# Decoder layer on one core: scaling of h on GpSimd and ScalarE, squares summed first, quarters of six column pairs ahead

## The chip, the cores and the metric

One core of a Trainium2 chip. The metric is the device time of one execution in microseconds (us), the median of three runs. In the text TensorE is PE in the rows, VectorE is DVE, ScalarE is ACT, GpSimd is POOL, and SyncE, which issues the weight loads, is SP.

## What is computed

One hybrid decoder layer on 256 tokens of width 2048, all in float32: a conditioning vector gives six modulation vectors, a normalised and modulated `h` feeds two token mixers (an attention with low-rank projections and an mLSTM), their gated sum goes through an output projection, and a mixture of 32 experts follows. The part that matters here is the beginning:

```python
mod = cond @ w_ada[l] + b_ada[l]
sh_a, sc_a, gt_a, sh_m, sc_m, gt_m = [m[:, None, :] for m in jnp.split(mod, 6, axis=-1)]
h = rmsnorm(x, norm_mix_g[l]) * (1.0 + sc_a) + sh_a
...
proj = h @ w_in
```

`rmsnorm(x, g)` is `x * rsqrt(mean(x * x) + EPS) * g`, and `w_in` is split into the columns of nine projections.

## The kernel before

Activations lie transposed: a block k holds 128 of the 2048 features on the partitions and 256 tokens along the free axis, so there are 16 blocks (`KT`). Weights come from HBM in pieces of 1 MB into the rotating buffers of the pool `big` (nine of them; conditioning vector and the halves of `h` hold some for long). SyncE issues the loads in the order of the program, and each waits until its buffer is free.

**Matmuls in parts.** Most products with `h` are made of three matmuls (`mm3`, L198 to L201): weights and activations are each split into a rounded high part (ScalarE, `split` L186, and `hh`) and a remainder (VectorE, L187, and `hl`). These are the split matmuls. In the first eight blocks (`WHOLE`) the head columns are multiplied in full float32 instead (L810), from `h` itself.

**The start.** ScalarE squares x in eight pieces, and TensorE sums each over the partitions by two products with a matrix of ones (L208); from the sum ScalarE makes `rstd`, the inverse root (L157, L158).

**The head loop** (from L787) goes over the 16 blocks. For block k it loads two rows of `w_ada` (1 MB each) and the head columns of `w_head` (0.7 MB); VectorE multiplies the two rows with the conditioning vector and sums along the free axis (`ada`, L143: a product of 128x2048 and a read of its accumulator), which gives the scale and the shift of the block; then come the gain (`ada_gain`, L151), the shift's bias (`ada_bias`, L146) and the scaling of x by gain and `rstd` (L805) on VectorE, the shift on ScalarE (L808), the high part (L811, ScalarE) and the remainder (L812, VectorE), and eleven products of 128x256 on TensorE. From block 8 on the head columns are split too (`push`), and behind each block stand some of 14 further pieces, `first_halves`: the first eight row blocks of six pairs of query and key columns (`half_pair`, 48 split matmuls each, tile `hp` in PSUM, copied to `part` by ScalarE, L322), of the mLSTM's values (`v_half`, tile `vb`) and of four pairs of output gates. At block 8 the program also emits `rope_tables`, 22 operations on GpSimd that start from the token positions (a load of its own, L348). The second halves are added to `part` later by VectorE (L328).

**What sets the order.** SyncE keeps the order of the program. On the other engines the compiler arranges the instructions at build time, and each engine then executes its list in that order. `push` runs one piece late, so that a split stands ahead of the matmuls that use it.

Of the kernel before, what the change touches and what calls it, by code (L numbers as in the profile page):

```python
# [9 lines left out]
F32 = mybir.dt.float32  # L10
# [63 lines left out]
def decoder_layer_kernel(ctx, tc, xT, c, pos, cols_d, const_d, mask_d, w_ada, w_head, w_half, w_blk, w_mlv, w_pa, w_pb, w_out,  # L74
# [11 lines left out]
    def bank(name):  # L86
        return psum.tile([P, 512], F32, name=name, tag="bank")
# [26 lines left out]
    def col(name, i=0, n=1, p0=0, p1=P):  # L114
        s = COLS[name].start + i
        return cols[p0:p1, s:s + n]
# [19 lines left out]
        act.activation(cond[:, s], b, AF.Silu)  # L136
    pool.memset(lg, NEG)
    vec.tensor_scalar(bada1, col("b_ada", 0, 96), 1.0, None, op0=ALU.add)

    def ada(i):  # L140
        raw = u8("raw")
# [5 lines left out]

    def ada_gain(which, k0, k1, base, g):
        s = slice(base + k0, base + k1)
        if k1 - k0 == 1:  # L150
            vec.tensor_scalar(gs[:, which, k0:k1], mod[:, s], bada1[:, s], col(g, k0), op0=ALU.add, op1=ALU.mult)  # L151
        else:
            vec.tensor_tensor(gs[:, which, k0:k1], mod[:, s], bada1[:, s], op=ALU.add)
            vec.tensor_tensor(gs[:, which, k0:k1], gs[:, which, k0:k1], col(g, k0, k1 - k0), op=ALU.mult)

    def rsqrt(out, ssum, n):
        act.activation(out, ssum, AF.Ln, bias=epsc, scale=1.0 / n)  # L157
# [20 lines left out]
    def pair(name, dt=F32):  # L178
        return by2(t2(name, dt))
# [20 lines left out]
        pe.matmul(out, wh, xl, start=False, stop=False)  # L200
        pe.matmul(out, wl, xh, start=False, stop=last)  # L201

    ssum = bank("ssum")
    for i in range(8):
        sq = pair("sq")
        act.activation(sq, xs[:, 2 * i:2 * i + 2], AF.Square)
        for j in range(2):
            pe.matmul(ssum[:, :T], ones, sq[:, j], start=i + j == 0, stop=i + j == 8)  # L208
    rstd = t2("rstd")
    rsqrt(rstd[:, :T], ssum[:, :T], D)  # L210

# [3 lines left out]
    def hhk(k):  # L215
        return hh[k // 8][:, k % 8]

    def hlk(k):
        return hl[k // 8][:, k % 8]
# [41 lines left out]
    def load(src):  # L261
        raw = u8("raw")
        nc.sync.dma_start(raw, src)
        return raw
# [24 lines left out]
    hblk = [hb[i // 2][:, (i % 2) * T:(i % 2 + 1) * T] for i in range(HEAD_N)]  # L289
    part = {}  # L290

    def half_pair(src, half, after):
        raw = load(src[half])
        b = bank("hp")
        for i in range(2):
            push_block(raw[:, i * 1024:(i + 1) * 1024], b[:, i * T:(i + 1) * T], 8, lambda k: hhk(k + 8 * half),
                       lambda k: hlk(k + 8 * half), (lambda: after(b)) if i else None)

    def v_half(nh, half, after):
        vb = [bank("vb") for _ in range(2)]  # L300
# [31 lines left out]

    def first_halves():
        for i in range(6):
            half_pair(w_half[i], 0, keep_part(("qk", i)))
            yield
        for nh in range(2):
            yield from v_half(nh, 0, keep_part(("v", nh, 0), ("v", nh, 1)))
        for i in range(4):
            half_pair(w_half[6 + i], 0, keep_part(("o", i)))  # L340
            yield
# [445 lines left out]
            push_block(raw[:, i * 1024:(i + 1) * 1024], b[:, i * T:(i + 1) * T], 8, pick(x, 0), pick(x, 1),  # L787
                       (lambda: after(b)) if i else None)

    firsts, n_first = first_halves(), 0  # L790
    for k in range(KT):
        ada(16 + k)
        ada(k)
        raw = u8("raw")[:, :HEAD_N * P]
        nc.sync.dma_start(raw, w_head[k])
        if k == 0:
            nc.sync.dma_start(const, const_d)
        if k == WHOLE:
            rope_tables()
        if k == KT - 1:  # L800
            nc.sync.dma_start(masks, mask_d)
        ada_gain(0, k, k + 1, 16, "mix_g")
        ada_bias(k, k + 1)
        hp = t2("hp")
        vec.scalar_tensor_tensor(hp[:, :T], xs[:, k], gs[:, 0, k:k + 1], rstd[:, :T], op0=ALU.mult, op1=ALU.mult)  # L805
        if k < WHOLE:
            h = hp[:, T:]
            act.activation(h, hp[:, :T], AF.Identity, bias=mod[:, k:k + 1])  # L808
            for j in range(HEAD_N):
                pe.matmul(hblk[j], raw[:, j * P:(j + 1) * P], h, start=k == 0 and j % 2 == 0, stop=False)  # L810
            act.activation(hhk(k), h, AF.Copy)  # L811
            vec.tensor_tensor(hlk(k), h, hhk(k).bitcast(F32), op=ALU.subtract)  # L812
            tick()
            tick()
            continue
        act.activation(hhk(k), hp[:, :T], AF.Identity, bias=mod[:, k:k + 1])
        vec.scalar_tensor_tensor(hlk(k), hp[:, :T], mod[:, k:k + 1], hhk(k).bitcast(F32), op0=ALU.add, op1=ALU.subtract)
        for j0, j1 in ((0, 6), (6, HEAD_N)):
            def fn(wh, wl, j0=j0, j1=j1, k=k):
                for j in range(j0, j1):  # L820
                    s = slice((j - j0) * P, (j - j0 + 1) * P)
                    mm3(hblk[j], wh[:, s], wl[:, s], hhk(k), hlk(k), k == 0 and j % 2 == 0,
                        k == KT - 1 and (j % 2 == 1 or j == HEAD_N - 1))

            push(raw[:, j0 * P:j1 * P], fn, after_head if k == KT - 1 and j1 == HEAD_N else None)
        while n_first < 14 * (k - 7) // 8:
            next(firsts)
            n_first += 1
# [639 lines left out]
def _layout(v):  # L1468
# [14 lines left out]
    head = np.concatenate([cq, ckv, kpe, mi, gap, mf, gap, mqk[:, :P * HEAD_QK]], 1).reshape(KT, P, HEAD_N * P)  # L1483
    two = np.concatenate([mqk[:, P * HEAD_QK:], mlo], 1)
    half = np.stack([blocks(two[:D // 2], 2), blocks(two[D // 2:], 2)], 1)
    blk = np.concatenate([blocks(ga), blocks(gb)], 0)
    mlv = mlv.reshape(4, 4, P, 2, 512).transpose(3, 0, 2, 1, 4).reshape(2, 4, P, 2048)
    uq = f("w_uq")[0].reshape(512, H, 192)
# [70 lines left out]
```

## Time and profile before

| what | before |
|---|---|
| median of 3 runs | 1639.17 us (1639.06 to 1639.73) |
| profiled execution | 1639.2 us, span 1637.3 us |
| TensorE busy | 1378.5 us, 84% |
| VectorE busy | 815.3 us, 50% |
| ScalarE busy | 504.2 us, 31% |
| GpSimd busy | 87.4 us, 5% |
| DMA | 560.96 MB, mean 343 GB/s |
| mean granted TensorE clock | 0.921 |

Busy shares are means over stages with different limits. TensorE's matmuls are pipelined, and a matmul that waits inside the pipeline still counts as busy; so the distance between the starts of matmuls, and the waits of the first one of a group, say more than the share. The granted clock is in parts of full speed: 1.00 is 2.4 GHz, 0.50 is 1.2 GHz.

### The profile page before, as it was taken

The page shows a single profiled execution, that of the slowest core. Times are in us where ns is not written, and L with a number is a line of the kernel's source. Part 1 is how long each engine was busy: PE and PEld are TensorE (multiplying, and loading weights), DVE is VectorE, ACT ScalarE, POOL GpSimd, SP SyncE. Part 2 cuts the span into 40 slices and gives each one's busy share as a digit, 9 for nine tenths or more (in the row PEclk, how much of TensorE's full clock was granted, in tenths as well). Part 3 has the DMA queues.
Part 4 walks back from the last instruction along what each step waited for, and adds up shares of the span by engine and source line. Part 5 has one row for each costly group of instructions (what it writes and reads, how often), then busy time and mean ns, then how long its engine had stood idle before and what let it go on. Part 6 is the DMA issues. An engine that isn't in the chain of part 4 may idle for free.

```text
span 1637.3 us, 24656 instructions
## 1 busy us (share of the span) xinstructions
PE 1378.5 (84%) x9726; PEld 1009.6 (62%) x9726; DVE 815.3 (50%) x1177; ACT 504.2 (31%) x720; POOL 87.4 (5%) x91
## 2 busy tenths in 40 slices
PE   7899998999999999999989689868767656657675
PEld 5698997999999989999747356535413213213212
DVE  5878699879776789986414233224301201201102
ACT  3134765446755574445312121212001001001000
POOL 0150014000000010121000000000000000000000
PEclk9899999999999999999999889998868878888888
DMA  9978767878676779874597999999999999999995
GB/s 383 374 283 329 282 212 283 327 286 296 245 273 242 269 267 416 321 297 155 224 409 273 416 400 378 420 417 393 399 421 422 420 422 421 420 422 421 421 421 228
DMA packets 78462, 560.96 MB, mean 343 GB/s; under 512 B 8705, under 2 KB 8961, under 8 KB 11905
## 3 DMA queue, kind: packets, MB, share of 16 engines
q1 hardware_dynamic: 78050, 558.84, 86.5%
q8 instruction: 80, 1.31, 0.3%
q10 hardware_dynamic: 288, 0.45, 0.1%
q14 instruction: 44, 0.36, 0.1%
HBM read 569.74 MB, written 2.10 MB: 349 GB/s over the span
## 4 chain that ended last, share of the span: by engine, by line
PE 50%; DMA 33%; DVE 6%; ACT 3%; issue 2%; POOL 1%; SPq 0%; DVEq 0%; POOLq 0%; ACTq 0%
DMA ring<-in_w_gu_dram 22%; DMA ring<-in_w_dn_dram 11%; PE gu L1285 6%; PE ga L199 4%; PE yb L1285 4%; PE ga L201 3%; PE ga L200 3%; DVE whl L187 2%; PE hp L201 2%; PE hp L199 2%; PE hp L200 2%; PE xb L1259 2%; PE wo L199 1%; DVE raw L143 1%; PE wo L201 1%
## 5 line engine op out<-in xcount | busy, mean ns | idle before, releaser
L1285 PE MATMUL gu<-ring,xg 128*32 128x512 f32 (+1 forms) x1664 | 270.4, 756 | 138.0 <-DMA ring<-in_w_gu_dram 138.0
L187 DVE TENSOR_TENSOR whl<-raw,whl 128x1024 fp32r<-128x1024 f32 (+1 forms) x222 | 267.1, 1210 | 93.1 <-ACT whl L186 92.6
L186 ACT ACTIVATE whl<-raw 128x1024 fp32r<-128x1024 f32 (+1 forms) x222 | 229.5, 1038 | 255.3 <-PE ga L201 62.7
L1285 PEld LDWEIGHTS gu<-ring,xg 128*32 128x32 f32 (+1 forms) x1664 | 65.7, 136 | 324.6 <-DMA ring<-in_w_gu_dram 172.0
L143 DVE SCALAR_TENSOR_TENSOR raw<-raw,cond 128x2048 f32<-128x2048 f32 x96 | 220.3, 2296 | 16.5 <-DMA raw<-in_w_ada_dram 16.4
L1285 PE MATMUL yb<-ring,aT 128*32 128x512 f32 (+1 forms) x832 | 130.7, 725 | 64.0 <-DMA ring<-in_w_dn_dram 61.9
L199 PE MATMUL ga<-hh,whl 128*128 128x256 f32 x512 | 149.6, 292 | 0.0
L201 PE MATMUL ga<-hh,whl 128*128 128x256 f32 x512 | 145.0, 283 | 1.4 <-DVE whl L187 1.3
L200 PE MATMUL ga<-hl,whl 128*128 128x256 f32 x512 | 144.8, 283 | 0.0
L1285 PEld LDWEIGHTS yb<-ring,aT 128*32 128x32 f32 (+1 forms) x832 | 33.5, 131 | 145.2 <-issue 99.6
L1231 DVE SCALAR_TENSOR_TENSOR xs<-ob,mod,xs 128x256 f32<-128x256 f32 x112 | 46.5, 477 | 131.9 <-PE ob L1325 131.9
L1251 DVE TENSOR_REDUCE wc<-cb 128x1 f32<-128x256 f32 x7 | 3.0, 424 | 215.8 <-PE cb L1248 215.8
L199 PEld LDWEIGHTS ga<-hh,whl 128*128 128x128 f32 x512 | 97.9, 191 | 5.1 <-issue 3.5
L201 PEld LDWEIGHTS ga<-hh,whl 128*128 128x128 f32 x512 | 97.9, 191 | 2.0 <-DVE whl L187 2.0
L200 PEld LDWEIGHTS ga<-hl,whl 128*128 128x128 f32 x512 | 98.0, 191 | 1.0 <-issue 0.7
L187 DVE TENSOR_TENSOR whl<-rawb,whl 128x1024 fp32r<-128x1024 f32 x36 | 43.0, 1221 | 110.7 <-ACT whl L186 110.7
L1303 ACT ACTIVATE s<-gu 128x512 f32<-128x512 f32 x7 | 4.2, 594 | 295.8 <-PE gu L1285 295.8
L201 PE MATMUL hp<-hh,whl 128*128 128x256 f32 x320 | 91.7, 287 | 3.4 <-DVE whl L187 3.3
L199 PE MATMUL hp<-hh,whl 128*128 128x256 f32 x320 | 92.6, 290 | 0.0
L200 PE MATMUL hp<-hl,whl 128*128 128x256 f32 x320 | 91.2, 285 | 0.0
L1314 ACT ACTIVATE yh<-yb 128x512 fp32r<-128x512 f32 x28 | 16.8, 599 | 190.2 <-PE yb L1285 190.2
L186 ACT ACTIVATE whl<-rawb 128x1024 fp32r<-128x1024 f32 x36 | 36.7, 1050 | 122.6 <-DMA rawb<-in_w_gu_dram 59.7
(418 smaller groups left out, 2905.6 us busy)
## 6 DMA issues: line engine op xcount, KB each, us to landing
ring<-in_w_gu_dram SPq DMA_DIRECT2D x208, 1024.0 KB, 14.8
ring<-in_w_dn_dram SPq DMA_DIRECT2D x104, 1024.0 KB, 15.1
raw<-in_w_ada_dram SPq DMA_DIRECT2D x96, 1024.0 KB, 6.8
raw<-in_w_blk_dram SPq DMA_DIRECT2D x32, 1024.0 KB, 5.1
raw<-in_w_half_dram SPq DMA_DIRECT2D x20, 1024.0 KB, 6.9
raw<-in_w_out_dram SPq DMA_DIRECT2D x16, 1024.0 KB, 6.5
raw<-in_w_head_dram SPq DMA_DIRECT2D x16, 704.0 KB, 7.8
rawb<-in_w_gu_dram SPq DMA_DIRECT2D x10, 1024.0 KB, 10.4
```

Of the source, the lines that this page charges most:

```text
L143: vec.scalar_tensor_tensor(raw, raw, 1.0, cond, op0=ALU.mult, op1=ALU.mult, accum_out=mod[:, i:i + 1])
L186: keep(act.activation(hi, raw, AF.Copy))
L187: keep(vec.tensor_tensor(lo, raw, hi.bitcast(F32), op=ALU.subtract))
L199: pe.matmul(out, wh, xh, start=first, stop=False)
L200: pe.matmul(out, wh, xl, start=False, stop=False)
L201: pe.matmul(out, wl, xh, start=False, stop=last)
L1231: vec.scalar_tensor_tensor(xs[:, d], src, mod[:, 80 + d:81 + d], xs[:, d], op0=ALU.mult, op1=ALU.add)
L1251: vec.tensor_reduce(wc, cb[:, :T], axis=AX.X, op=ALU.add)
L1259: pe.matmul(b[:, i * P:(i + 1) * P], xr[tt][:, k * P:(k + 1) * P], gt[tt], start=tt == 0, stop=tt == 1)
L1285: return lambda: pe.matmul(out[j * C:(j + 1) * C, :], x[:, k * P + j * C:k * P + (j + 1) * C], ws[j][:, cut], start=first, stop=stop)
L1303: act.activation(s, gu[0], AF.Silu)
L1314: act.activation(yh, yb, AF.Copy)
```

## The change

Three things are changed.

First, the eight squared pieces are added up on VectorE, and only the sum goes through the products with ones: two instead of sixteen.

Second, in the head loop the three operations on VectorE (gain, bias, scaling) are gone. GpSimd multiplies x with `rstd`, which needs no conditioning; ScalarE makes the gain (as `mod * mix_g + gbias`, with `gbias` made once) and the biased shift, and applies both in one activation. The high part and the remainder of a block are made in the same way in all 16 blocks.

Third, `half_pair` takes quarters: its 1 MB of weights is laid out so that half of it holds four row blocks of both columns. Six quarters (row blocks 0 to 3) run inside the loop behind blocks 4 to 7: one, two, one and two. `first_halves` then runs only row blocks 4 to 7 of these six pairs, and VectorE adds them to `part`.

```diff
+    gbias = keep.tile([P, KT], F32, name="gbias")
+    vec.tensor_tensor(gbias, bada1[:, KT:2 * KT], col("mix_g", 0, KT), op=ALU.mult)
...
-    ssum = bank("ssum")
+    ssum, total = bank("ssum"), None
     for i in range(8):
-        sq = pair("sq")
-        act.activation(sq, xs[:, 2 * i:2 * i + 2], AF.Square)
-        for j in range(2):
-            pe.matmul(ssum[:, :T], ones, sq[:, j], start=i + j == 0, stop=i + j == 8)
+        sq = t2("sq")
+        act.activation(by2(sq), xs[:, 2 * i:2 * i + 2], AF.Square)
+        if total is None:
+            total = sq
+        else:
+            vec.tensor_tensor(total, total, sq, op=ALU.add)
+    for j in range(2):
+        pe.matmul(ssum[:, :T], ones, total[:, j * T:(j + 1) * T], start=j == 0, stop=j == 1)
...
-    def half_pair(src, half, after):
-        raw = load(src[half])
+    def half_pair(src, half, after, quarters=(0, 1)):
+        q0, q1 = quarters[0], quarters[-1] + 1
+        raw = u8("raw")[:, :(q1 - q0) * 1024]
+        nc.sync.dma_start(raw, src[half][:, q0 * 1024:q1 * 1024])
         b = bank("hp")
-        for i in range(2):
-            push_block(raw[:, i * 1024:(i + 1) * 1024], b[:, i * T:(i + 1) * T], 8, lambda k: hhk(k + 8 * half),
-                       lambda k: hlk(k + 8 * half), (lambda: after(b)) if i else None)
+        for q in quarters:
+            def fn(wh, wl, q=q):
+                for i in range(2):
+                    for j in range(4):
+                        k, s = 8 * half + 4 * q + j, slice((4 * i + j) * P, (4 * i + j + 1) * P)
+                        mm3(b[:, i * T:(i + 1) * T], wh[:, s], wl[:, s], hhk(k), hlk(k), q == q0 and i + j == 0,
+                            q == q1 - 1 and i == 1 and j == 3)
+            push(raw[:, (q - q0) * 1024:(q - q0 + 1) * 1024], fn, (lambda: after(b)) if q == q1 - 1 else None)
+
+    def quarter(i):
+        half_pair(w_half[i], 0, keep_part(("qk", i)), (0,))
...
         for i in range(6):
-            half_pair(w_half[i], 0, keep_part(("qk", i)))
+            half_pair(w_half[i], 0, add_part(("qk", i)), (1,))
...
-        ada_gain(0, k, k + 1, 16, "mix_g")
-        ada_bias(k, k + 1)
         hp = t2("hp")
-        vec.scalar_tensor_tensor(hp[:, :T], xs[:, k], gs[:, 0, k:k + 1], rstd[:, :T], op0=ALU.mult, op1=ALU.mult)
+        h = hp[:, T:]
+        pool.tensor_tensor(hp[:, :T], xs[:, k], rstd[:, :T], op=ALU.mult)
+        act.activation(gs[:, 0, k:k + 1], mod[:, 16 + k:17 + k], AF.Identity, bias=gbias[:, k:k + 1], scale=col("mix_g", k))
+        act.activation(mod[:, k:k + 1], mod[:, k:k + 1], AF.Identity, bias=col("b_ada", k))
+        act.activation(h, hp[:, :T], AF.Identity, bias=mod[:, k:k + 1], scale=gs[:, 0, k:k + 1])
+        act.activation(hhk(k), h, AF.Copy)
+        vec.tensor_tensor(hlk(k), h, hhk(k).bitcast(F32), op=ALU.subtract)
         if k < WHOLE:
...
+            if k >= 4:
+                while n_quarter < 6 * (k - 3) // 4:
+                    quarter(n_quarter)
+                    n_quarter += 1
             continue
-        act.activation(hhk(k), hp[:, :T], AF.Identity, bias=mod[:, k:k + 1])
-        vec.scalar_tensor_tensor(hlk(k), hp[:, :T], mod[:, k:k + 1], hhk(k).bitcast(F32), op0=ALU.add, op1=ALU.subtract)
```

How this moves instructions is seen at four places; the lists are the compiled order of an engine, one row per instruction or run of equal ones. On VectorE at the start, after the change: `sq` is the running sum of squares, `raw,mod<-raw,cond` the conditioning product of a row.

```order
L209 TENSOR_TENSOR sq<-sq 128x512 x4
L145 SCALAR_TENSOR_TENSOR raw,mod<-raw,cond 128x2048
L209 TENSOR_TENSOR sq<-sq 128x512 x2
L145 SCALAR_TENSOR_TENSOR raw,mod<-raw,cond 128x2048
L209 TENSOR_TENSOR sq<-sq 128x512
L822 TENSOR_TENSOR hl<-hp,hh 128x256
```

The last addition stands behind the two products of block 0; before, no addition stood there.

On GpSimd, after the change, around block 8: `hp<-xs,rstd` is the new scaling of a block, `pf`, `kq`, `uq` and `pi` are tiles of the rope tables, and `pi` holds the positions.

```order
L817 TENSOR_TENSOR hp<-xs,rstd 128x256 x8
L363 CAST pf<-pi 128x256
L365 TENSOR_SCALAR pf<-pf,cols 128x256
L369 TENSOR_SCALAR kq<-pf 128x256
...
L375 TENSOR_SCALAR trig<-kq 128x256
L372 TENSOR_SCALAR uq<-kq 128x256
L817 TENSOR_TENSOR hp<-xs,rstd 128x256
L373 TENSOR_TENSOR kq<-uq,pf 128x256
L817 TENSOR_TENSOR hp<-xs,rstd 128x256
```

The scalings of blocks 0 to 7 come first; that of block 8 stands behind 15 operations of the rope tables, and those of blocks 9 to 15 between the remaining ones. Before, GpSimd's list held only the rope tables here, and the scaling was VectorE's.

On ScalarE, after the change, from block 4 to block 6: `whl<-raw` is the high part of a quarter's weights, `part<-hp 128x512` the copy of a quarter out of PSUM, `gs`, `mod`, `hp<-hp,mod,gs` and `hh` the gain, shift, application and high part of the next block.

```order
L185 ACTIVATE whl<-raw 128x1024
L818 ACTIVATE gs<-mod,gbias,cols 128x1
L335 ACTIVATE part<-hp 128x512
L819 ACTIVATE mod<-mod,cols 128x1
L820 ACTIVATE hp<-hp,mod,gs 128x256
L821 ACTIVATE hh<-hp 128x256
L185 ACTIVATE whl<-raw 128x1024 x2
L818 ACTIVATE gs<-mod,gbias,cols 128x1
L335 ACTIVATE part<-hp 128x512 x2
L819 ACTIVATE mod<-mod,cols 128x1
```

A quarter's copy stands ahead of the next block's shift. Before, ScalarE's list in these blocks held only the shift and the high part.

On VectorE, after the change, from the remainder of block 8 to that of block 9: `part<-hp,part` is the sum of a pair's two quarters, `whl<-raw,whl 128x768` and `128x640` the remainders of block 9's head weights.

```order
L822 TENSOR_TENSOR hl<-hp,hh 128x256
L145 SCALAR_TENSOR_TENSOR raw,mod<-raw,cond 128x2048
L186 TENSOR_TENSOR whl<-raw,whl 128x1024
L145 SCALAR_TENSOR_TENSOR raw,mod<-raw,cond 128x2048
L341 TENSOR_TENSOR part<-hp,part 128x512
L186 TENSOR_TENSOR whl<-raw,whl 128x768
L186 TENSOR_TENSOR whl<-raw,whl 128x640
L822 TENSOR_TENSOR hl<-hp,hh 128x256
```

The sum of the quarters waits for TensorE and stands in this stretch, where before the block's scaling and gain stood and no sum.

## Rows read from the trace of the kernel before

**Rows 1.** The chain of waits that ended last, shares of the span by engine.

```profile
PE 50%; DMA 33%; DVE 6%; ACT 3%; issue 2%; POOL 1%; SPq 0%; DVEq 0%; POOLq 0%; ACTq 0%
```

**Rows 2.** Stretches: us, busy (x instructions) per engine, granted clock, DMA share, GB/s.

```profile
40.00:60.00 20.00, 17.74 (x71) 14.32 (x70) 16.61 (x24) 2.77 (x6) 0.00 (x0) 0.90 0.99 391
...
80.00:85.00 5.00, 5.00 (x26) 5.00 (x25) 1.78 (x2) 2.02 (x2) 4.58 (x6) 0.52 0.93 387
...
137.00:186.00 49.00, 48.09 (x313) 43.64 (x312) 38.30 (x48) 23.93 (x33) 0.00 (x0) 1.00 0.93 352
```

**Rows 3.** Timeline, block 1: start, duration, instruction, [idle before, releaser].

```profile
22.63 2.29 DVE L143 SCALAR_TENSOR_TENSOR raw<-raw,cond 128x2048 f32<-128x2048 f32 x1
...
24.96 0.27 DVE L151 TENSOR_SCALAR gs<-mod,bada,cols 128x1 f32<-128x1 f32 x1
25.27 0.48 DVE L805 SCALAR_TENSOR_TENSOR hp<-xs,gs,rstd 128x256 f32<-128x256 f32 x1
...
28.00 0.16 DVE L146 TENSOR_TENSOR mod<-mod,cols 128x1 f32<-128x1 f32 x1
...
28.75 5.01 PE L810 MATMUL hb<-hp,raw 128*128 128x256 f32 x22 [1.88 <-ACT hp L808]
...
29.52 2.28 DVE L143 SCALAR_TENSOR_TENSOR raw<-raw,cond 128x2048 f32<-128x2048 f32 x1
```

**Rows 4.** Timeline of TensorE, blocks 8 and 9 and the first `vb`.

```profile
78.96 0.80 PE L199 MATMUL hb<-hh,whl 128*128 128x256 f32 x2 [3.83 <-ACT hh L816]
...
93.37 1.25 PE L199 MATMUL hb<-hh,whl 128*128 128x256 f32 x6 [1.81 <-ACT hh L816]
...
136.67 0.40 PE L311 MATMUL vb<-whl,hh 128*128 128x512 f32 x1
```

**Rows 5.** Timeline of TensorE, split matmuls at the two clocks.

```profile
80.71 0.41 PE L200 MATMUL hb<-hl,whl 128*128 128x256 f32 x1
...
80.92 0.41 PE L201 MATMUL hb<-hh,whl 128*128 128x256 f32 x1
...
85.64 0.28 PE L199 MATMUL hp<-hh,whl 128*128 128x256 f32 x1
...
85.76 0.28 PE L200 MATMUL hp<-hl,whl 128*128 128x256 f32 x1
```

**Rows 6.** Timeline of the start.

```profile
9.59 8.92 PE L208 MATMUL ssum<-sq,ones 128*128 128x256 f32 x32
...
12.28 2.29 DVE L143 SCALAR_TENSOR_TENSOR raw<-raw,cond 128x2048 f32<-128x2048 f32 x1 [9.02 <-DMA raw<-in_w_ada_dram]
```

**Rows 7.** Costliest groups: count, busy us, mean ns, idle before: the splits.

```profile
L187 DVE TENSOR_TENSOR whl<-raw,whl 128x1024 fp32r<-128x1024 f32 (+1 forms) x222 | 267.1, 1210 | 93.1 <-ACT whl L186 92.6
L186 ACT ACTIVATE whl<-raw 128x1024 fp32r<-128x1024 f32 (+1 forms) x222 | 229.5, 1038 | 255.3 <-PE ga L201 62.7
```

**Rows 8.** Lines L328 and L322: duration ns min/median/max, first and last start.

```profile
L328 DVE TENSOR_TENSOR part<-hp,part x10: 679/685/692, 211.0 to 329.7; 128x512 f32<-128x512 f32 x10
L322 ACT ACTIVATE part<-hp x10: 579/598/600, 91.6 to 205.2; 128x512 f32<-128x512 f32 x10
```

**Rows 9.** Timeline of GpSimd, operations 1, 7, 8, 12 and 15 of the rope tables.

```profile
76.12 0.90 POOL L350 CAST pf<-pi 128x256 f32<-128x256 int32 x1 [75.24 <-DMA pi<-in_pos_dram]
...
82.89 0.85 POOL L359 TENSOR_SCALAR uq<-kq 128x256 f32<-128x256 f32 x1
83.83 0.73 POOL L360 TENSOR_TENSOR kq<-uq,kq 128x256 f32<-128x256 f32 x1
...
89.30 3.00 POOL L361 TENSOR_SCALAR kq<-kq 128x256 f32<-128x256 f32 x1
...
94.70 1.19 POOL L359 TENSOR_SCALAR uq<-kq 128x256 f32<-128x256 f32 x1
```

**Rows 10.** Timeline of SyncE, the issue of the positions.

```profile
66.69 0.42 SPq L348 DMA_DIRECT2D pi<-in_pos_dram  x1
```

More of the change, by code (lines that the diff above doesn't have):

```diff
@@ L149, in ada_gain @@
         s = slice(base + k0, base + k1)
[L150 to L154, printed above, removed]
+        vec.tensor_tensor(gs[:, which, k0:k1], mod[:, s], bada1[:, s], op=ALU.add)
+        vec.tensor_tensor(gs[:, which, k0:k1], gs[:, which, k0:k1], col(g, k0, k1 - k0), op=ALU.mult)
     def rsqrt(out, ssum, n):
@@ L788, in proj_gemm @@
                        (lambda: after(b)) if i else None)
-    firsts, n_first = first_halves(), 0
+    firsts, n_first, n_quarter = first_halves(), 0, 0
     for k in range(KT):
@@ L801, in decoder_layer_kernel @@
             nc.sync.dma_start(masks, mask_d)
-        ada_gain(0, k, k + 1, 16, "mix_g")
-        ada_bias(k, k + 1)
         hp = t2("hp")
-        vec.scalar_tensor_tensor(hp[:, :T], xs[:, k], gs[:, 0, k:k + 1], rstd[:, :T], op0=ALU.mult, op1=ALU.mult)
+        h = hp[:, T:]
[5 more added lines that the diff above has]
+        vec.tensor_tensor(hlk(k), h, hhk(k).bitcast(F32), op=ALU.subtract)
         if k < WHOLE:
-            h = hp[:, T:]
-            act.activation(h, hp[:, :T], AF.Identity, bias=mod[:, k:k + 1])
             for j in range(HEAD_N):
                 pe.matmul(hblk[j], raw[:, j * P:(j + 1) * P], h, start=k == 0 and j % 2 == 0, stop=False)
-            act.activation(hhk(k), h, AF.Copy)
-            vec.tensor_tensor(hlk(k), h, hhk(k).bitcast(F32), op=ALU.subtract)
             tick()
             tick()
+            if k >= 4:
+                while n_quarter < 6 * (k - 3) // 4:
+                    quarter(n_quarter)
+                    n_quarter += 1
             continue
-        act.activation(hhk(k), hp[:, :T], AF.Identity, bias=mod[:, k:k + 1])
-        vec.scalar_tensor_tensor(hlk(k), hp[:, :T], mod[:, k:k + 1], hhk(k).bitcast(F32), op0=ALU.add, op1=ALU.subtract)
         for j0, j1 in ((0, 6), (6, HEAD_N)):
@@ L1485, in _layout @@
     half = np.stack([blocks(two[:D // 2], 2), blocks(two[D // 2:], 2)], 1)
+    half = np.ascontiguousarray(half.reshape(10, 2, P, 2, 2, 512).transpose(0, 1, 2, 4, 3, 5)).reshape(10, 2, P, 2048)
     blk = np.concatenate([blocks(ga), blocks(gb)], 0)
```

## The prediction

> **What bounds the kernel now.** I read the chain of waits first, then busy time by stretches, then the timeline of the stretch that the diff touches. The profiled execution took 1639.2 us with a span of 1637.3, so 1.9 us lie around the span; the median of the three runs is 1639.17, and I make the sum against 1639.2. About 0.2%, 3.3 us, is what a measurement of this kernel can tell from no change.
>
> The chain [rows 1] is half TensorE and a third DMA, the DMA part being the expert stage at the end. Everything that the diff touches lies before 137 us. From 137 to 186 us TensorE is busy for 48.09 of 49 us at a granted clock of 1.00 [rows 2], and nothing there waits long; the stages behind it follow from its end. So a delay or a gain in the first 137 us arrives at the end almost one to one, and the question is only when TensorE reaches its first `vb` matmul, which starts at 136.67 us now [rows 4].
>
> Ahead of that TensorE loses time in two ways. In the first eight blocks VectorE sets the pace: one block runs from 22.63 to 29.52 us, 6.89 us [rows 3], with two conditioning products, three small operations and a wait for ScalarE in it, while TensorE works 5.0 us of it and then waits 1.88. DMA is nearly as tight: share 0.99 from 40 to 60 us at 391 GB/s [rows 2]. Then, at the ninth block, TensorE waits 3.83 us until 78.96, and 1.81 more until 93.37 [rows 4]. After a wait it runs at the lower clock: in 80 to 85 us the granted clock is 0.52 [rows 2], that is mostly 1.2 GHz, and split matmuls start 0.21 us apart; from 85 us on, at 2.4 GHz, they start 0.12 us apart [rows 5]. From 78.96 to 136.67 us it issues four split blocks (132 matmuls) and six first halves (288): 420 times 0.12 is 50.4 us of the 57.7. So 7.3 us are lost there.
>
> **The start.** Sixteen products with `ones` go (8.92 us in 32 records, 0.28 each [rows 6]) and two stay, 4 records, 1.1 us. But the last of the seven new additions stands on VectorE behind both products of the first block, as the order shows. The first product starts when its weights land, 12.28 [rows 6]; two products of 2.35 and three additions of 0.65 (an addition of that shape takes 0.68 [rows 8], starting a little closer) end at about 19.2. With 1.1 us of `ones`, the same 2.2 us of ScalarE as now, 0.73 for POOL's scaling (the shortest two-input POOL row [rows 9]) and 0.5 for ScalarE, TensorE's first block starts at 24.0 instead of 21.86: **2.1 us later**. This part gives nothing back, because those products were hidden beside the conditioning weights.
>
> **Blocks 1 to 4.** VectorE loses 0.27, 0.48 and 0.16 us per block [rows 3]. Its block would be two products of 2.33 start to start, then ScalarE's shift, scale and copy, about 6.3 us. DMA does not follow: 2.8 MB per block at the present rate leaves about 6.7. So 0.2 us per block come back, and h of the fifth block (k = 4) is ready near 50.2 us against 48.9 now.
>
> **Quarters.** One is 24 split matmuls, 24 x 0.12 = 2.9 us at 2.4 GHz; six are 17.3 us of TensorE work taken from behind the ninth block. On ScalarE each quarter's copy out of PSUM (0.60 us [rows 8]) stands ahead of the next block's shift and scale, so the next block cannot start before the quarter ends: 0.6 + 0.2 + 0.5, about 1.4 us of idle TensorE. By that: block 4 at 50.7 to 55.7, quarter to 58.6; block 5 at 60.0 to 65.0, two quarters to 70.8; block 6 at 72.2 to 77.2, quarter to 80.1; block 7 at 81.5 to 86.5, two quarters to **92.3**. Splits and weights for these fit beside it (1.04 us on ScalarE and 1.21 on VectorE per quarter [rows 7], 3 MB more DMA in a stretch that is now longer). At the present rate the same work would stand at 78.96 + 17.3 = 96.2, so up to here the change is 3.9 us ahead.
>
> **The wait that I expect.** The scaling of block k = 8 is now on POOL, and in POOL's order it stands behind 15 operations of the rope tables. Those start when the positions land: 76.12 now, 9.4 us behind their issue [rows 9, 10]. With the change that issue follows the weights of k = 8, whose buffers wait for block 6 on TensorE (77.2), so the positions land near 86.9. The 15 operations took from 76.12 to 95.9, 19.8 us, with VectorE working beside them; rows that met an idle VectorE took 0.73 and 0.85 [rows 9], which makes 12.7 for 15. I take **12.7**, because VectorE itself soon stands still: its next operation but a few is the lower part of the same block. So scaling at 99.6 to 100.3, ScalarE's two steps to 101.3: TensorE starts block 8 at **101.3**, after 9 us of waiting, 5.1 behind 96.2.
>
> No row shows a POOL operation that is ready held behind one that isn't. The Trainium skill (TensorE: Matmul & The Clock Gate, section Architectural detail) says that GpSimd takes instructions strictly first in, first out on each of its cores. By it the sum stays as it is; if it did not hold, block 8 would start at 93.7, which is the second rival below.
>
> A POOL scaling took 0.73 us in its nearest row where VectorE's takes 0.48 [rows 3, 9]. The skill (GPSIMD Engine Reference, Engine selection) advises VectorE for such work and calls GpSimd about twice as slow with two inputs. By that 0.96 would stand for 0.73, and the sum would grow by 0.5 us, for the first block and block 8.
>
> **Behind block 8.** After a wait of 9 us I charge the lower clock again, as at 78.96: block 8 takes 6.5 us instead of 4.0, to 107.8, quarter to 110.7. VectorE's order has the sum of that quarter ahead of the product of block 9, so 0.65 + 2.35 us there, then 0.2 + 0.65 + 0.5 + 1.05 + 0.4 on ScalarE, where two splits stand between: block 9 starts near 116.6 after 5.9 us, and again slowly, to 123.1. Two quarters to 128.9, block 10 to 132.9, two quarters to 138.7; there two sums and the split of block 11 on VectorE cost some 3 us; block 11 and the last quarter to 148.2. First `vb` at **148.2** against 136.67: 11.5 us. Small things: ScalarE's six copies are the same six as now; the six sums (4.1 us) and the gain taken off VectorE (0.9 us per block) lie beside TensorE from 137 us on, at nothing, as TensorE is the bound there; without that cover eight blocks would gain 7.3 us on VectorE and the sums cost 4.1.
>
> Sum: 1639.2 + 11.5 = 1650.7; I say **1651**.
>
> **Rivals.**
> 1. *The rope operations run as slowly as now* (19.8 us): block 8 starts at 108.4, everything 7.1 later: 1658. For it: the 3.00 us row that lay across a product on VectorE [rows 9]. Against it: VectorE mostly waits. 15%.
> 2. *POOL holds nothing back* (the positions land early, or the scaling is not behind them): block 8 at 93.7 (92.3 + 1.4) at the full clock saves 7.6 + 2.5 of the sum: about 1640.6, no change. For it: the positions are 128 small rows, and nothing forces them behind the weights except their place. Against: they took 9.4 us in the same place. 17%.
> 3. *It works as meant*: POOL in time, and the quarters keep TensorE fed from 50 us on, with no wait at blocks 9 and 11. From 93.7 only 132 + 144 matmuls remain, 33.1 us: first `vb` at 126.8, **1629**, 9.9 us faster. It decides this way if the positions land before about 78 us and the additions on VectorE do not stand ahead of the products in time. For it: 7.3 us are lost now in that stretch. Against: both orders. 8%.
>
> **How the numbers follow.** The forecast has 60%. Its own range, from positions that land 3 us earlier or later and one more or one fewer slow restart of 2.5 us, is 1645 to 1656. With the first rival above and the second below, the range is 1636 to 1659; it leaves out the third and some tails. Slower by over 0.2%: forecast and first rival, 0.75. Within 0.2%: the second, 0.17. Faster: 0.08.
>
> **What would show it.** In the timeline of POOL: the first eight scalings back to back near 23 us, then nothing until the positions land at 84 to 89 us, and the ninth behind the rope operations. In TensorE's waits: one of 6 us or more at block 8, ended by ScalarE's copy of h, and a second of 4 to 6 us at block 9; a granted clock near 0.5 behind each. VectorE's small operations gone and its blocks at 6.4 to 6.8 us before the fifth. TensorE's first block at 24 us. The time of the stages from `vb` on should be unchanged. If block 8 starts before 95 us, or the first `vb` before 138 us, the prediction is wrong in its main step; if block 8 starts late and the end does not move, something behind 137 us had slack that I did not see.

## The result and the profile after

The changed kernel took 1658.12 us (median of 4 runs, 1654.45 to 1661.57) beside 1639.45 (1639.06 to 1640.79) for the kernel before on the same chip: a ratio of 1.011, 95% interval 1.0091 to 1.013. It is slower. The profiled execution took 1654.45 us with a span of 1652.6; it is the shortest of the four, 3.7 us below their median, so the times read from its trace below add up to less than the difference of the medians.

TensorE's list of work is shorter (1359.2 us busy, 1378.5 before), and yet the chain that ended last holds more of "issue" than in [rows 1], which is time in which an engine waited for nothing that the profile shows (it is not traced further here):

```profile
PE 1359.2 (82%) x9698; PEld 1000.2 (61%) x9698; DVE 812.1 (49%) x1143; ACT 517.3 (31%) x760; POOL 100.7 (6%) x107
PE 48%; DMA 34%; DVE 6%; issue 6%; ACT 3%; POOL 2%; SPq 0%; DVEq 0%; POOLq 0%; ACTq 0%
```

The timeline of the start, where [rows 6] stood: the first conditioning product, the last addition of squares, the ones products, the first eight scalings on GpSimd, a conditioning product beside them, and TensorE's blocks 0 and 4.

```profile
13.48 2.29 DVE L145 SCALAR_TENSOR_TENSOR raw<-raw,cond 128x2048 f32<-128x2048 f32 x1
...
19.30 0.69 DVE L209 TENSOR_TENSOR sq<-sq 128x512 f32<-128x512 f32 x1
20.04 2.08 PE L211 MATMUL ssum<-sq,ones 128*128 128x256 f32 x4 [9.95 <-DVE sq L209]
24.44 9.78 POOL L817 TENSOR_TENSOR hp<-xs,rstd 128x256 f32<-128x256 f32 x8 [23.56 <-ACT rstd L157]
25.85 7.22 PE L825 MATMUL hb<-hp,raw 128*128 128x256 f32 x22 [3.73 <-ACT hp L820]
26.73 2.81 DVE L145 SCALAR_TENSOR_TENSOR raw<-raw,cond 128x2048 f32<-128x2048 f32 x1
...
52.70 5.02 PE L825 MATMUL hb<-hp,raw 128*128 128x256 f32 x22 [1.33 <-ACT hp L820]
```

The timeline around block 8, where [rows 4, 9, 10] stood:

```profile
81.89 0.45 SPq L361 DMA_DIRECT2D pi<-in_pos_dram  x1
89.29 0.81 POOL L363 CAST pf<-pi 128x256 f32<-128x256 int32 x1 [55.08 <-DMA pi<-in_pos_dram]
90.22 2.84 POOL L365 TENSOR_SCALAR pf<-pf,cols 128x256 f32<-128x256 f32 x1
...
105.04 0.72 POOL L817 TENSOR_TENSOR hp<-xs,rstd 128x256 f32<-128x256 f32 x1
105.80 0.60 ACT L820 ACTIVATE hp<-hp,mod,gs 128x256 f32<-128x256 f32 x1 [10.48 <-POOL hp L817]
106.90 0.79 PE L198 MATMUL hb<-hh,whl 128*128 128x256 f32 x2 [12.22 <-ACT hh L821]
116.45 0.69 DVE L341 TENSOR_TENSOR part<-hp,part 128x512 f32<-128x512 f32 x1 [4.65 <-PE hp L200]
121.79 0.58 PE L198 MATMUL hp<-hh,whl 128*128 128x256 f32 x1 [5.38 <-ACT whl L185]
...
154.25 0.40 PE L324 MATMUL vb<-whl,hh 128*128 128x512 f32 x1
```

GpSimd begins the rope tables when the positions land, and only then does it reach the scaling of block 8, 15.7 us later; TensorE stands for 12.22 us, where it stood for 3.83 [rows 4]. Behind the wait TensorE is slow again (columns as in [rows 2]):

```profile
106.00:110.00 4.00, 3.10 (x14) 3.04 (x15) 2.70 (x3) 1.76 (x3) 3.92 (x5) 0.50 0.02 4
122.00:126.00 4.00, 4.00 (x18) 3.70 (x19) 3.34 (x3) 0.05 (x1) 0.26 (x1) 0.51 1.02 397
```

The first `vb` comes 17.6 us later than before. The first product of the attention gates (`ga`), after the whole first part, is 17.5 us later (346.4 against 328.9), and the last `yb`, at the end of the expert stage, 15.2 (1636.9 against 1621.7). So what is lost ahead of `vb` is the loss.

### The profile page after: what moved, and what is told of

The parts are those of the page before. It is cut to its first block, busy times and chain, and to the rows that moved or that the text cites. A ratio compares the mean times of both kernels' runs of the same rounds, so it can differ in the third digit from the quotient of the medians.

```text
span 1652.6 us, 24679 instructions
## 1 busy us (share of the span) xinstructions
PE 1359.2 (82%) x9698; PEld 1000.2 (61%) x9698; DVE 812.1 (49%) x1143; ACT 517.3 (31%) x760; POOL 100.7 (6%) x107
## 4 chain that ended last, share of the span: by engine, by line
PE 48%; DMA 34%; DVE 6%; issue 6%; ACT 3%; POOL 2%; SPq 0%; DVEq 0%; POOLq 0%; ACTq 0%
DMA ring<-in_w_gu_dram 24%; DMA ring<-in_w_dn_dram 10%; PE gu L1300 6%; PE ga L198 4%; PE ga L200 4%; PE ga L199 4%; PE yb L1300 3%; DVE whl L186 2%; PE xb L1274 2%; PE hp L198 2%; PE hp L200 2%; DVE raw L145 2%; PE hp L199 2%; PE wo L198 1%; PE wo L200 1%
## 5 line engine op out<-in xcount | busy, mean ns | idle before, releaser
L145 DVE SCALAR_TENSOR_TENSOR raw<-raw,cond 128x2048 f32<-128x2048 f32 x96 | 221.1, 2308 | 12.8 <-DMA raw<-in_w_ada_dram 12.5
L1300 PE MATMUL yb<-ring,aT 128*32 128x512 f32 (+1 forms) x832 | 125.3, 696 | 64.8 <-DMA ring<-in_w_dn_dram 62.8
## 6 DMA issues: line engine op xcount, KB each, us to landing
ring<-in_w_dn_dram SPq DMA_DIRECT2D x104, 1024.0 KB, 15.2
```

What stands on the lines that cost most here:

```text
L145: vec.scalar_tensor_tensor(raw, raw, 1.0, cond, op0=ALU.mult, op1=ALU.mult, accum_out=mod[:, i:i + 1])
L1300: return lambda: pe.matmul(out[j * C:(j + 1) * C, :], x[:, k * P + j * C:k * P + (j + 1) * C], ws[j][:, cut], start=first, stop=stop)
```

## The experiments

Two landmarks are used for all runs: the starts of the first `vb` and of the first `ga` product. The ratio is against the kernel before, run on the same chip. Times of landmarks are from one execution of each kernel. In the runs without a wait for the query squares (below), the stretch from the first `vb` to the first `ga` took 190.8 to 195.7 us, at a granted clock of 0.97 to 0.99, although nearly the same work stands there; so a difference of 2 us at `ga` tells little, and the ratio and both landmarks have to be read together.

| kernel | ratio, 95% interval | first vb | first ga |
|---|---|---|---|
| before | 1 | 136.7 | 328.9 |
| the change | 1.011, 1.0091 to 1.013 | 154.3 | 346.4 |
| squares alone | 1.0004, 0.9993 to 1.0014 | 138.4 | 329.4 |
| scaling alone | 1.0078, 1.0052 to 1.0104 | 151.3 | 343.5 |
| quarters alone | 1.0064, 1.0044 to 1.0084 | 140.9 | 334.0 |
| change, scaling on VectorE | 1.0064, 1.0047 to 1.0081 | 141.0 | 335.4 |
| change, rope spread | 1.0054, 1.0037 to 1.0071 | 143.3 | 337.8 |
| change, rope last | 1.0145, 1.0114 to 1.0176 | 146.2 | 354.4 |
| change, old squares | 1.0116, 1.0085 to 1.0147 | 151.3 | 346.0 |
| change, rope last, old squares | 1.0121, 1.0088 to 1.0154 | 142.0 | 348.4 |
| change, no quarters | 1.0082, 1.0051 to 1.0113 | 155.1 | 347.4 |
| before, rope early | 0.9986, 0.9971 to 1.0001 | 136.2 | 327.0 |
| quarters, rope early | 1.0045, 1.0028 to 1.0062 | 143.4 | 337.5 |
| quarters, rope early, sum on GpSimd | 1.004, 1.0022 to 1.0058 | 141.6 | 337.3 |

### Where the rope tables stand

Rope tables last: emitted behind the scaling of block 15.

```diff
-        if k == WHOLE:
-            rope_tables()
         hp = t2("hp")
...
         pool.tensor_tensor(hp[:, :T], xs[:, k], rstd[:, :T], op=ALU.mult)
+        if k == KT - 1:
+            rope_tables()
```

> The changed kernel with the rope tables emitted behind the scaling of the last block, so that GpSimd's list holds all sixteen scalings first. Theory 1 (GpSimd holds block 8 back): the wait of 12.2 us at block 8 falls to under 3 us, block 8 starts at 95 to 97 us instead of 106.9 and keeps the full clock, the first vb comes near 141 us instead of 154.3, and the time is near 1645 us. Rival (the late blocks 4 to 7 with their quarters are the cost, and TensorE would next wait for the split of block 8's weights): block 8 starts after 102 us and the time stays above 1652.

Block 8's wait fell from 12.22 to 2.10 us and `vb` came 8.1 us earlier. All sixteen scalings now ran back to back from 24.23 us on, the ninth at 33.98; in the change, the ninth ran at 105.04. So what it needs was there some 70 us earlier, and the rope operations did hold it. But the time did not fall to 1645 us, as the first theory had it: `ga` came 8.0 us later than in the change, and the ratio is 1.0145 (the two intervals overlap). The timeline of the scalings, of block 8 and of the new end of the rope tables, and the waits of TensorE from 184 to 232 us (total, times, longest):

```profile
24.23 23.82 POOL L815 TENSOR_TENSOR hp<-xs,rstd 128x256 f32<-128x256 f32 x16 [23.35 <-ACT rstd L157]
...
99.07 0.98 PE L198 MATMUL hb<-hh,whl 128*128 128x256 f32 x6 [2.10 <-ACT hh L821]
...
184.87 0.74 SPq L361 DMA_DIRECT2D pi<-in_pos_dram  x1
194.20 0.40 POOL L363 CAST pf<-pi 128x256 f32<-128x256 int32 x1 [146.15 <-DVE hl L822]
...
213.63 0.85 POOL L375 TENSOR_SCALAR trig<-kq 128x256 f32<-128x256 f32 x1
214.45 1.26 POOL L418 TENSOR_TENSOR sq<-sq 128x512 f32<-128x512 f32 x1
```

```profile
PE st L422 <- POOL sq L418: 13.9, 1, 13.9
```

The same 22 operations now hold another one: the sum of the query squares (L418), for which TensorE waits 13.9 us. A wait was moved, not removed.

Rope tables spread: `rope_tables` made a generator, a few operations per block behind that block's scaling.

```diff
+        if k:
+            next(rope_steps, None)
```

> The changed kernel with the 22 rope operations issued a few at a time from the second row block on, between the scalings on POOL, so that they are neither ahead of the scaling of block 8 when it is wanted nor behind that of block 15. Theory 1 (POOL's order makes the loss, twice: rope operations ahead of the scalings hold block 8 by 12 us, and rope operations behind all scalings held the sum of the q squares, for which PE stood 13.9 us in the run with the rope tables last): block 8 begins by 100 us after a wait of about 2 us, the first vb product at about 146, PE waits under 2 us for the sum of the q squares, the first ga product comes at about 340 instead of 354, and the time is 14 us under the run with the rope tables last, about 1650 us, ratio 1.003 to 1.006. Rival (where the rope operations stand does not matter, the longer chain on ScalarE does): block 8 still waits 9 us or more and the ratio stays at 1.009 to 1.012.

```profile
97.63 1.65 PE L198 MATMUL hb<-hh,whl 128*128 128x256 f32 x6 [2.10 <-ACT hh L826]
```

With nothing behind or ahead of them that is wanted, both waits are gone: `ga` came 16.6 us earlier than with the rope tables last, the ratio fell to 1.0054. That is the first theory's number, and still slower than before.

### Each part alone

The change with its old ones products (first block at 22.52 instead of 25.85):

> The changed kernel with the sixteen products of ones of the kernel before. Theory (the last addition behind two products sets the start): the first block starts at 22 to 22.5 us instead of 25.85, all that follows comes 3 to 4 us earlier, time near 1654 us against 1658. Rival (the blocks behind it are held by the DMA of the conditioning weights, so an early start is lost by block 3): block 4 starts within 1 us of now (52.7) and the time is unchanged.

The start's 3.3 us were 3.0 at block 4 (49.67), 3.0 at `vb` and 0.4 at `ga`, and the ratio is no lower (1.0116). So the rival's time held, though not its reason. Between `vb` and `ga` nothing differs in the program; the stretches from the first copy of the head's results (tile `cq`) to `ga`, of the change and then of this run, do:

```profile
203.30:346.40 143.10, 136.48 (x971) 126.13 (x969) 125.85 (x153) 89.04 (x121) 24.50 (x22) 0.99 0.74 264
200.80:346.00 145.20, 138.55 (x972) 128.18 (x970) 126.11 (x153) 89.08 (x121) 24.50 (x22) 0.96 0.72 259
```

The granted clock was lower here (0.96 against 0.99), and the stretch is 2.1 us longer. The same with the rope tables last:

> Rope tables last and the old sixteen products, in the changed kernel: what is left is the quarters and the scaling on GpSimd and ScalarE. If the two causes add up: first vb near 137 us and 1640 to 1642 us, the kernel before's time, with the stall at block 9 (5.4 us, VectorE's sum ahead of the conditioning product) still there. If the quarters pay beside that: 1632 to 1637.

Again the hold was gone (block 8 at 96.27 after 2.10 us), and again TensorE waited for the query squares, 12.8 us; `vb` came at 142.0, and neither of the two times expected came out (1661.69 us). Squares alone, in the kernel before:

> The kernel before with the squares summed ahead of two pairs of ones products, and nothing else. Theory 1 (the start is 3.5 to 4 us later, and a part fades where loads set the pace): first block at 25 to 26 us, block 8 at 80 to 83, first vb at 138 to 141, ratio 1.001 to 1.0025. Rival (the loads that went on meanwhile give all of it back, as the change with its old ones products, only 0.4 us ahead at the first ga product, would have it): first vb under 137.5, ratio 0.999 to 1.001.

```profile
25.23 12.18 PE L814 MATMUL hb<-hp,raw 128*128 128x256 f32 x44 [3.35 <-ACT hp L812]
82.30 0.50 PE L199 MATMUL hb<-hh,whl 128*128 128x256 f32 x2 [1.92 <-ACT hh L820]
```

The first block is 3.4 us late and block 8 still 3.3, but its wait is 1.9 us shorter than [rows 4]; `vb` is 1.7 late, `ga` 0.5, and the time the same within its interval. The rival's time held, although `vb` did as the first theory said. What gave the delay back can be read from block 8 itself, in the kernel before and then here (columns as in [rows 2]):

```profile
78.96:85.80 6.84, 6.84 (x35) 6.82 (x36) 3.04 (x4) 2.12 (x2) 6.33 (x7) 0.57 0.86 359
82.30:86.80 4.50, 4.48 (x35) 4.28 (x36) 2.31 (x3) 1.95 (x2) 4.16 (x5) 1.00 0.98 411
```

After 3.83 us of waiting the block ran at a granted clock of 0.57 and took 6.8 us; after 1.92 us it ran at 1.00 and took 4.5. From `vb` to `ga` the clock was a little higher again (0.99 against 0.98), and the stretch 1.2 us shorter. So what was regained of the start's delay was regained, for the most part, by TensorE's clock.

Scaling alone (GpSimd and ScalarE; squares and pairs as before):

> The kernel before with the scaling of h alone as changed (product on POOL, gain, shift and rounding on ScalarE, rope operations on POOL at their old place); squares and column pairs as before. Theory 1 (the hold on POOL is a loss by itself): the rope operations run from about 76 to 92 us ahead of the scaling of block 8, block 8 begins at 92 to 95 us after a wait of 14 us or more, first vb product at 148 to 152, ratio 1.005 to 1.009. Rival (the hold costs only together with the quarters or the later start): block 8 before 86 us, first vb under 142, ratio under 1.003.

```profile
92.69 0.80 PE L198 MATMUL hb<-hh,whl 128*128 128x256 f32 x2 [16.87 <-ACT hh L817]
```

So the scaling on GpSimd, with the hold, is a loss by itself: 14.6 us at both landmarks, where block 8's wait is 13.0 us longer than [rows 4]. The change with that one product back on VectorE:

```diff
-        pool.tensor_tensor(hp[:, :T], xs[:, k], rstd[:, :T], op=ALU.mult)
+        vec.tensor_tensor(hp[:, :T], xs[:, k], rstd[:, :T], op=ALU.mult)
```

> The changed kernel with the one scaling of h per row block on VectorE instead of POOL (0.4 to 0.5 us each); rope operations alone on POOL at their old place; squares summed ahead and quarters stay. Theory 1 (the hold on POOL is the larger part of the loss): block 8 begins at about 97 us after a wait of at most 4 us, blocks 2 and 3 take no longer than the others, the first vb product comes at 143 to 147, the first ga product at 335 to 341, ratio 1.001 to 1.005. Rival (VectorE, busy with the ada products, holds the scaling back as much as POOL does): block 8 waits 8 us or more again, first vb at 152 or later, ratio 1.008 or more.

```profile
96.04 0.50 PE L198 MATMUL hb<-hh,whl 128*128 128x256 f32 x2 [2.15 <-ACT hh L821]
```

`vb` came 13.3 us earlier than in the change and `ga` 11.0, as the first theory had it; the ratio, 1.0064, is above its bound of 1.005. So more than the hold was lost.

### The quarters

The change without quarters:

> The changed kernel without the six quarters: the six pairs run all eight row blocks behind block 8, as before the change. Theory 1 (GpSimd's list): still slow. Blocks 4 to 7 take 6.4 us each, the positions land at 78 to 81 us, block 8 starts at 94 to 97 us after a wait of 14 us or more, and first vb is at 151 to 154 us: time 1653 to 1657. Rival (the quarters cost what the change costs): first vb at 137 to 140 us and the time within 4 us of the kernel before.

Still slower than before, and block 8 waits 16.52 us. Whether the quarters help or hurt inside the change stays unclear: `ga` is 1.0 us later without them, the ratio lower, and the intervals overlap. Quarters alone answer better:

> The kernel before with the quarters alone (six column pairs run their first four row blocks from the fifth on); squares and scaling of h as before. Theory 1 (the loads fill the first stage already, so the quarters only move both their loads and their 17.3 us of products ahead of block 8 and gain little): blocks 4 to 7 take 9 to 12 us instead of 6.7, block 8 begins at 90 to 94 us after a wait of 4 to 8 us, the first vb product comes at 134 to 140 (136.7 before), ratio 0.998 to 1.003. Rival (works as meant): block 8 by 90 us with a wait under 3 us, first vb at 126 to 131, ratio 0.993 to 0.996.

They lose 5.1 us at `ga`, and both expectations missed: the ratio is 1.0064, where the first theory had at most 1.003 and the rival a gain. The stretches from block 4 to block 8 and from block 8 to `vb`, of the kernel before and then with quarters:

```profile
49.40:79.00 29.60, 23.48 (x89) 18.75 (x89) 25.05 (x35) 5.17 (x10) 2.67 (x3) 0.87 0.93 369
79.00:136.70 57.70, 55.50 (x421) 54.78 (x422) 42.23 (x48) 23.08 (x28) 25.01 (x19) 0.92 0.81 300
```

```profile
50.60:92.70 42.10, 37.27 (x232) 34.19 (x232) 32.34 (x41) 14.03 (x23) 3.33 (x4) 1.00 0.93 364
92.70:140.90 48.20, 39.70 (x276) 38.27 (x277) 36.93 (x44) 14.15 (x17) 24.75 (x19) 0.86 0.78 276
```

The first stretch grows by 12.5 us for some 17 us of products: that side works. The second shrinks by only 9.5, as TensorE is busy for 39.70 of 48.20 where it was busy for 55.50 of 57.70, and the granted clock is 0.86. Its longest wait stands behind a sum of quarters on VectorE:

```profile
101.63 0.69 DVE L338 TENSOR_TENSOR part<-hp,part 128x512 f32<-128x512 f32 x1 [4.02 <-PE hp L201]
...
106.24 1.22 PE L199 MATMUL hb<-hh,whl 128*128 128x256 f32 x4 [4.65 <-ACT hh L830]
```

So two causes were tried: the rope operations beside it, and the sum.

> The kernel before with the quarters and with the rope tables at the second row block, so that no rope operation runs beside blocks 8 to 11. Theory 1 (the quarters lose because the sum of a second quarter on VectorE waits for PE, 4.02 us at 101.6 in the run with quarters alone, ahead of the ada product, the gain and the scaling of the next block): only the ada products beside rope operations get shorter (2.8 to 2.3 us), block 9 still waits 3 to 5 us, first vb at 138 to 141, ratio 1.003 to 1.0065. Rival (the rope operations beside these blocks are the loss): block 9 waits under 2 us, first vb at 132 to 136, ratio 0.996 to 1.000.

The second run has the edits of this one and the following:

```diff
+    def pool_part(key):
+        def after(b):
+            t = t2("pp")
+            act.activation(t, b, AF.Copy)
+            pool.tensor_tensor(part[key], part[key], t, op=ALU.add)
+        return after
...
-            half_pair(w_half[i], 0, add_part(("qk", i)), (1,))
+            half_pair(w_half[i], 0, pool_part(("qk", i)), (1,))
```

> As the kernel before with quarters and early rope tables, but a second quarter is copied out of PSUM by ScalarE (0.6 us, as a whole half was before) and added to the first on POOL, where nothing waits behind it: no sum stands on VectorE ahead of the next block. Theory 1 (the sum on VectorE is the loss): blocks 9 to 11 wait under 2 us each, first vb at 130 to 136, ratio 0.994 to 1.000. Rival (the cover is the loss: with half of the products gone from between the heads of blocks 8 to 13, VectorE's ada products and splits set the pace there, whoever adds): blocks 9 to 11 still wait 3 us or more together with VectorE busy throughout, first vb at 138 to 141, ratio 1.003 to 1.0065.

Neither took the loss away: 1.0045 and 1.004, beside 1.0064 with intervals that overlap, and `ga` at 337.5 and 337.3, later than the 334.0 of the quarters alone. Part of that is the early rope tables, which make the early blocks longer (block 8 starts at 95.42 and 94.90 us, and at 92.71 with the quarters alone). Beside the kernel before with the same early rope tables (below, 0.9986 and `ga` at 327.0), the quarters lose more, not less. With the rope tables early, block 9 still waits 4.43 us. Without the sum on VectorE it waits 1.81, but the next blocks wait longer in its place (2.59 and 1.70 us at the heads of blocks 10 and 11), as the rival had it. VectorE is not busy throughout, as the rival had said it would be: 37 of the 47 us from block 8 to `vb`. The timeline of that run ahead of block 11:

```profile
123.72 1.06 ACT L186 ACTIVATE whl<-raw 128x1024 fp32r<-128x1024 f32 x1 [4.71 <-PE hb L201]
124.81 1.22 DVE L187 TENSOR_TENSOR whl<-raw,whl 128x1024 fp32r<-128x1024 f32 x1 [3.62 <-ACT whl L186]
125.95 2.28 DVE L143 SCALAR_TENSOR_TENSOR raw<-raw,cond 128x2048 f32<-128x2048 f32 x1
...
128.47 2.28 DVE L143 SCALAR_TENSOR_TENSOR raw<-raw,cond 128x2048 f32<-128x2048 f32 x1
130.68 1.49 DVE L822 SCALAR_TENSOR_TENSOR hp<-xs,gs,rstd 128x256 f32<-128x256 f32 x1
...
130.86 0.28 PE L201 MATMUL hp<-hh,whl 128*128 128x256 f32 x1
132.27 0.51 ACT L837 ACTIVATE hh<-hp,mod 128x256 fp32r<-128x256 f32 x1 [2.59 <-DVE mod L146]
132.84 0.39 PE L199 MATMUL hb<-hh,whl 128*128 128x256 f32 x1 [1.70 <-ACT hh L837]
```

A chain leads round all engines: TensorE frees a buffer for split weights (123.72), ScalarE and VectorE fill it, and only then VectorE comes to the two conditioning products, the scaling and so to the next `hh`, 8.6 us later. About 1 us of it is this run's own doing: the scaling took 1.49 us beside GpSimd's sum of quarters, and 0.48 in [rows 3]. Within that time TensorE has the rest of a block and two quarters of 2.9 us, and runs out at about 131.1. Before, whole first halves of 5.8 us (48 times 0.12) stood there. That this chain is the quarters' loss is argued from the rows, and not shown: a run that shortens it (a fourth buffer for split weights, where the kernel has three, or conditioning products ahead of the split) was not made.

### The rope tables early, in the kernel before

```diff
-        if k == WHOLE:
+        if k == 1:
             rope_tables()
```

> The kernel before with the rope tables issued at the second row block instead of the ninth, so that POOL's 22 operations and the load of the positions lie between about 20 and 55 us and not at 76 to 97. Theory 1 (operations on POOL cost the kernel only through what waits behind them or runs beside them): nothing waits behind them here; the ada products beside them, now 2.48 to 2.8 us instead of 2.28, move to the first stage, where loads set the pace; the waits ahead of blocks 8 and 9 (3.88 and 1.81 us) shrink by 0 to 3 us; first vb at 134 to 137; ratio 0.998 to 1.000. Rival (the ada products in the first stage become the limit and blocks 1 to 3 get longer by 1 us each): first vb at 138 to 140, ratio 1.001 to 1.002.

The time is within the interval of no change (0.9986, up to 1.0001). Block 8's wait shrinks to 1.93 us, but the block begins 2.2 us later, at 81.16, as early blocks got longer. No version was found that is faster than the kernel before beyond doubt.

## Why the prediction was right, and where not

**The sign and the main step** were right: the scaling of block 8 behind 15 rope operations is the largest part. The second rival put its price at 7.6 + 2.5 = 10.1 us at the first `vb`. Taking the hold away gave 11.0 us there with the rope tables spread and 13.3 with the scaling on VectorE; of the latter 11.0 were left at `ga`, and in time 1.011 - 1.0064, about 7.5 us. That GpSimd holds a ready operation behind one that isn't, which no row showed then, the runs with another order on GpSimd show: the ninth scaling ran at 33.98 us instead of 105.04. The rule of the Trainium skill (TensorE: Matmul & The Clock Gate, Architectural detail) agrees with that.

**The time** was 7 us too low: 1651 forecast, 1658.12 measured. That lies within the range only because the first rival had widened it; the forecast's own range ended at 1656. And it is the first rival's number by luck: that rival had the rope operations at 19.8 us and all else as forecast, and they took 15.7. At `vb` the profiled execution is 6.0 us behind the forecast (154.25 and 148.2), and nearly all of it stood at block 8, which began at 106.90 instead of 101.3. Two terms of the sum made this.

- *The positions* landed 2.4 us late, at 89.29. Block 6 ended at 79.48 instead of 77.2, mostly because the first block had begun 1.9 us later than forecast. That the positions were no later than that is luck: their issue came at 81.89, 4.4 us behind the 77.5 that the forecast implies, and the positions then took 7.4 us and not 9.4.
- *The 15 rope operations* took 15.7 us instead of 12.7. Two of them met VectorE at work, although VectorE was said to stand still soon: 2.84 and 1.68 us, where the same two took 0.93 and 1.10 at the new end of the run with the rope tables last. That is 2.5 of the 3.0 us.

From block 8 to `vb` the forecast of 46.9 us was met with 47.4.

**The start** was mis-sized. It was 4.0 us late, not 2.1. The terms given (12.28 + 2 x 2.35 + 3 x 0.65) make 18.9 and not 19.2, and with the rest 23.5 and not 24.0. Measured, the first conditioning product stood behind additions until 13.48, the last addition ended at 19.99, and the four ones records took 2.08 us, not 1.1, after 9.95 us of nothing on TensorE (the 0.28 us a record of [rows 6] is a mean of two speeds, see the last section). What lay behind the start was met: from the first block to block 4 it was 26.85 us, 6.7 a block, as forecast. (2.8 MB at the 391 GB/s of [rows 2] would be 7.2; the 6.7 came from no row.) What failed is that a delay in the first 137 us "arrives at the end almost one to one": for the squares alone, 3.4 us at the first block were 0.5 at `ga`.

**The scaling's price** of 0.73 us on GpSimd held where VectorE stood (0.72). Beside the first conditioning products it did not: two of the first eight scalings took 2.77 us, which makes 1.22 in the mean (9.78 / 8), and the products became 2.81 us in turn. The Trainium skill (GPSIMD Engine Reference, Engine selection) calls GpSimd about twice as slow for such an operation. The same line took 0.42 us on VectorE in the run with the scaling there, so the trace has 1.7 times. The rows of the change and then of that run (ns, min/median/max):

```profile
L817 POOL TENSOR_TENSOR hp<-xs,rstd x16: 719/734/2770, 24.4 to 121.4; 128x256 f32<-128x256 f32 x16
L817 DVE TENSOR_TENSOR hp<-xs,rstd x16: 409/421/952, 24.3 to 98.1; 128x256 f32<-128x256 f32 x16
```

**The quarters** hold the step that failed. Blocks 4 to 7 went as worked out (1.56 us of idle after each where 1.4 was said). Alone, too, the quarters put TensorE about as far ahead at block 8 as the forecast said: 92.71, where 78.96 + 17.3 is 96.3. But they cost 5.1 us at `ga`, and the reason given for that was wrong: the waits behind block 8 were laid to the sum on VectorE, and with the sum elsewhere they came back in other blocks. The third rival, "it works as meant" at 1629 us, asked for positions in time and no sum ahead of the products. In the kernel before, quarters with both took 1.004 times as long as none. The whole change with both was not run.

**Do the parts add up?** Alone they cost 0.5, 14.6 and 5.1 us at `ga`, 20.2 together; the change costs 17.5. The quarters hide part of the hold: block 8 waits 12.22 us with them and 16.52 in the change without them.

## What to carry to other kernels

Before an operation is moved to an engine that looks idle, read what stands ahead of it in that engine's list and when that can start. What is moved away from there can hold whatever comes behind its new place. Moving work forward out of a stage in which TensorE is full pays only if the stage can then run shorter: look for what that work was covering, here probably the chain from a freed buffer round to the next operand. And a delay early in a program need not arrive: measure each part alone.

## What the runs showed of the hardware

- A granted clock of 1.00 at the start can mean that nothing was recorded. The trace of the change holds no clock record before 30.35 us, and such a stretch prints as 1.00. The ones products, and block 0 until then, took 634 ns a record; from 30.35 us on it is 380. In the run with the quarters alone, which has records there, block 0 took 631 ns a record at 0.50 and 379 at 1.00; the stretches of both are shown below. In the kernel before, whose records begin at 13.16 us, the ones products turned from 634 to 379 ns just then. So TensorE most likely ran at 1.2 GHz at these starts.

```profile
22.80:28.40 5.60, 5.60 (x13) 4.48 (x14) 5.11 (x6) 0.39 (x1) 0.00 (x0) 0.50 0.86 357
28.50:33.00 4.50, 4.50 (x22) 3.96 (x21) 3.40 (x7) 0.92 (x2) 0.00 (x0) 1.00 0.28 83
```

- GpSimd and VectorE slow each other down. A scaling on GpSimd took 0.72 us, and 2.77 where it lay across a conditioning product; that product took 2.81 us instead of 2.28. A scaling on VectorE took 0.48 us, and 1.49 beside a sum on GpSimd.
- The expert stage, which no kernel here touches, took 852.0 us from the last `wo` to the last `yb` in one run (791.6 to 1643.6, rope tables last) and 861.9 in another (785.4 to 1647.3, with old squares too). Differences of a few us in the whole time are therefore less telling than the landmarks ahead of that stage.
